# Differential attention maps in three PSUM banks, and re-costed attention plans, in a two-block fp32 network

## The chip, the cores and the metric

One core of one Trainium2 chip. The metric is device microseconds of one execution. The program is one launch of some 52,000 instructions; everything is fp32 (matmuls run on fp32 data, in part split into a high and a low fp32r half).

## The reference, cut to what matters

The network is a first block (latent attention, dilated attention, an expert-choice feed-forward) and a second block of two layers. Each layer of the second block runs three attentions over 1024 positions and 256 context positions; the one that the change touches is the differential one, with 4 heads and two maps to a head:

```python
def diff_attend(q, k, v, lam):
    s = jnp.einsum('bqhmd,bkhmd->bhmqk', q, k).astype(jnp.float32) * (q.shape[-1] ** -0.5)
    p = jax.nn.softmax(s, axis=-1)
    a = (p[:, :, 0] - lam * p[:, :, 1]).astype(v.dtype)
    return jnp.einsum('bhqk,bkhd->bqhd', a, v)

for l in range(DEPTH_2):
    ...
    oa = map_query_blocks(lambda q_blk: diff_attend(q_blk, ka_all, va_all, lam), qa)
    yb = map_query_blocks(lambda q_blk: gqa_attend(q_blk, kb_all, vb_all), qb) * jax.nn.silu(gb)
    yn = neighbourhood_attend(qn, kn, vn, kn_c, vn_c, nat_rpb[l], rows)
    y = jnp.concatenate([ya, yb, yn], axis=-1) @ w_out[l]
    if l < DEPTH_2 - 1:
        ...   # the same for the 256 context rows, of layer 0 alone
```

With 128 queries to a tile, a layer has 4 heads x 8 tiles x 2 maps = 64 maps of 128 x 1280 scores.

## The kernel before

The program runs in stages: projections of the first block, its attention (`attn1`), its output projection and router, the experts, and for each of the two layers projections (`proj2`), attention (`attn2`) and output projection (`out2`). The three attention stages are not written in the order in which they run. They are handed to a planner, class `Plan`: `Plan.op` takes a priority, a dictionary of engines with an assumed duration in us on each (of several the first one that is free in the plan is taken), the function that emits the instructions, the operations it depends on, its buffers and the time of its transfer. `Plan.run` is a list scheduler: it walks through the assumed time, starts the ready operation of lowest priority number whose engine is free and whose buffers are to be had, and emits its instructions. Each engine then executes its instructions in the order so made. A dependency between engines counts `HOP`, and a load is done 2.0 us after its transfer. So the assumed durations set the order of the instructions and the choice between engines, and nothing else.

PSUM has eight banks of 512 fp32 columns. The tags `s` (scores), `t` (transposes and transposed scores) and `o` (outputs) share them, each up to a cap from the table `TUNE`; a buffer is taken in the plan when its first operation starts and given back when its last one ends.

A layer's plan has two streams. Stream `x` (`stream_x`) runs the neighbourhood attention of three pairs of heads and then grouped-query attention of three pairs; stream `d` (`stream_d`) the four differential heads. Each stream paces its priorities with `step`; `df` in `TUNE` stretches or shortens the pace of `d` as a share of the stage, `d0` is its start, `lead` is how far ahead loads are put, `aS`, `aD` and `aN` how far ahead the scores are put, `pvx` and `pvd` how far behind the products with the values.

A differential query tile (`d_tile`, line 2010) computes two maps. Its scores go to five `s` banks: two banks of 512 columns for each map, and one bank that holds the last 256 columns of both. For each piece VectorE copies the scores to SBUF and takes their maximum at once (`copy_max`, line 1859: the scores plus a broadcast zero, with an accumulated maximum). A small reduction (line 2038) makes the negated maximum of a map out of its three pieces, and ScalarE takes the exponential of all 1280 columns in place (line 2044) with that as bias. The second map, scaled by -lambda and the ratio of the sums, is added to the first on GpSimd or VectorE (`combine`, lines 1958 to 1961); ten transposes, their evictions and the product with the values follow.

A neighbourhood tile (`nat_tile`) takes two `s` banks and up to three passes with bias and maximum on VectorE (lines 2271 and 1861). Grouped-query attention and the latent attention of the first block (`st_group`) take the maxima of scores (line 1020), then scores anew in transposed form, exponentials on ScalarE (line 1053) and a running sum of them on GpSimd or VectorE (line 1057). The weights of the output projection are loaded and split inside the plan (`out2_weights`), once all four differential heads are done, as they take the space of the heads' buffers.

Of the kernel before, what the change touches and what calls it, by code (L numbers as in the profile page):

```python
# [9 lines left out]
F32 = mybir.dt.float32  # L10
# [78 lines left out]
class Plan:  # L89
# [4 lines left out]
    HOP = 0.22  # L94
# [60 lines left out]
    def run(self):  # L155
# [5 lines left out]
        while left:  # L161
# [11 lines left out]
            for o in cand:  # L173
# [17 lines left out]
                if o.dma:  # L191
                    dma = max(end, dma) + o.dma
                    done = dma + 2.0
# [18 lines left out]
        self.span = max(max(free.values()), dma + 2.0)  # L212
# [13 lines left out]
class Kern:  # L226
# [251 lines left out]
    def matvec_ops(self, p, dur, parts):  # L478
# [6 lines left out]
        for k in range(KD):  # L485
# [3 lines left out]
            o = pl.op(q, {"pe": 1.2}, lambda e, k=k, W=W: products(O.t, W.t, k), [lw, o], [W, O])  # L489
# [445 lines left out]
    def plan(self, caps, pools, rest):  # L935

        self.pl = pl = Plan(caps, BANKS)

        def buf(tag, stream, shape=None, dt=F32):
            if tag in ("t", "o", "oT"):  # L940
                stream = None
            if tag in ("s", "t", "o"):
                return pl.buf(tag, stream, lambda i: self.ps.tile([P, 512], F32, name=self.nm(tag), tag=f"b{i}", bufs=1))
# [5 lines left out]
    def mla_pair(self, p):  # L949
# [19 lines left out]
        def part(g):  # L969
# [3 lines left out]
            for i in range(2):  # L973
# [14 lines left out]
                fins.append(self.st_group(X, 3.05, NT, CH[:2], s1, st, 0.65, [Q, K], [lq, lk], Q, lambda Q=Q: Q.t[96:100, 0, :],  # L988
# [5 lines left out]
    def st_group(self, X, dur, nb, ch, s1, st, cost, QK, lds, M, mdst, V, lv, vc, Y, yc, tagP, tagA, sm):  # L994
# [7 lines left out]
        def tile_tops(pp, j0):  # L1002
# [4 lines left out]
            def bank(parts):  # L1007
# [14 lines left out]
                o = pl.op(p - self.q["aS"], {"pe": 0.02 + n * w * 0.00042}, mm, lds, [Sb] + QK)  # L1022
                os.append(pl.op(p - self.q["aS"], {"dve": 0.07 + n * w * 0.00104}, top, [o], [Sb]))
# [8 lines left out]
            tops.append(pl.op(pp[1] - self.q["aS"], {"dve": 0.08}, fin, os))  # L1032
# [14 lines left out]
        om = pl.op(p, {"act": 0.66, "dve": 0.6}, mrows, [o] + lds, [T, M])  # L1047
        exps, acc = [], None
        for kb in range(nb):
# [3 lines left out]
            exps.append(pl.op(q, {"act": 0.48}, lambda e, kb=kb, T_=T_: nc.scalar.activation(PT.t[:, kb, :], T_.t, AF.Exp), [o], [T_, PT]))  # L1053
            if kb:
# [3 lines left out]
                acc = pl.op(q, {"pool": 1.23, "dve": 0.6}, add, [exps[kb - 1], exps[kb], acc], [PT, A])  # L1058
# [62 lines left out]
    def dil_unit(self, p, h, part, half, Q, K, lds, Y, env):  # L1121
# [15 lines left out]
        def bank(a):  # L1137
# [20 lines left out]
            o = pl.op(p - self.q["aE"], {"pe": 0.43}, scores, lds, [Sb, Q, K])  # L1158
            tops.append(pl.op(p, {"dve": 0.68}, top, [o], [Sb, Pt] + yb))
# [1332 lines left out]
```

## Time and profile before

| | us |
|---|---|
| median of the runs (3593.01 to 3593.92) | 3593.58 |
| the profiled execution | 3575.55 |
| its span, first to last instruction | 3573.6 |
| busy in the span: TensorE (matmul) | 3341.9 (94%) |
| VectorE | 2359.4 (66%) |
| ScalarE | 1703.9 (48%) |
| GpSimd | 1221.0 (34%) |

Busy shares are averages over stages with different limits; the rows further below are by stage. Matmuls are pipelined and their ends are modelled, so TensorE's share says little about its rate; where it matters, the distance from the start of one matmul to the start of the next is read.

### The profile page before, as it was taken

The numbers are of one execution on the slowest core, as the hardware profiler recorded it, in microseconds if no ns is written. First come the engines' busy times: TensorE is split into PE (matmuls) and PEld (weight loads), VectorE is DVE, ScalarE is ACT, GpSimd is POOL, SyncE is SP. The second block draws the span as 40 slices with busy tenths as digits, with TensorE's granted clock in tenths as the row PEclk, the third lists the DMA queues.
The fourth block names the chain that finished last, engine by engine and source line by source line (L and its number), as shares of the span: only waits on it lengthen the run. The fifth ranks groups of instructions, "written<-read, shape, count | busy, mean of one in ns | idle before, by whom it ended". The sixth has DMA issues, their size and how long they took to land. (4 is left out here: it accounts for less than half of the span.)

```text
span 3573.6 us, 51656 instructions
## 1 busy us (share of the span) xinstructions
PE 3341.9 (94%) x17880; PEld 2572.3 (72%) x17880; DVE 2359.4 (66%) x5555; ACT 1703.9 (48%) x3138; POOL 1221.0 (34%) x1071
## 2 busy tenths in 40 slices
PE   7998899979499999989999899999999999999999
PEld 5987666657388887779889566556899888665557
DVE  5524546444799999876850788886546813899962
ACT  4324444422388877663321676554333213766540
POOL 3211323332000101033540356665334512556551
PEclk9999999999699999999999999999999999999999
DMA  7338677565799999654451653113344444531133
GB/s 206 92 112 234 159 211 218 162 217 180 256 393 392 399 392 362 235 169 127 134 156 55 159 124 86 38 40 124 124 128 128 116 142 115 145 89 45 40 101 112
DMA packets 398650, 600.21 MB, mean 168 GB/s; under 512 B 77330, under 2 KB 281234, under 8 KB 394290
## 3 DMA queue, kind: packets, MB, share of 16 engines
q1 hardware_dynamic: 339828, 486.92, 40.7%
q0 software_dynamic: 26240, 94.13, 11.3%
q10 hardware_dynamic: 32320, 15.86, 1.6%
q8 instruction: 141, 2.31, 0.3%
q14 instruction: 121, 0.99, 0.1%
HBM read 473.33 MB, written 123.50 MB: 167 GB/s over the span
## 5 line engine op out<-in xcount | busy, mean ns | idle before, releaser
L348 PE MATMUL a<-wh,h2H 128*128 128x384 f32 (+2 forms) x1328 | 475.5, 358 | 3.5 <-ACT h2H L595 3.5
L350 PE MATMUL a<-wh,h2L 128*128 128x384 f32 (+2 forms) x1328 | 469.1, 353 | 4.4 <-POOL h2L L596 4.3
L349 PE MATMUL a<-wl,h2H 128*128 128x384 f32 (+2 forms) x1328 | 468.6, 353 | 1.7 <-DVE wl L335 1.2
L1481 DVE TENSOR_TENSOR wl<-wr,wh 128x1024 fp32r<-128x1024 f32 x384 | 450.4, 1222 | 27.3 <-ACT wh L1480 20.8
L1480 ACT ACTIVATE wh<-wr 128x1024 fp32r<-128x1024 f32 x384 | 395.9, 1059 | 78.7 <-PE s L350 78.2
L350 PEld LDWEIGHTS a<-wh,h2L 128*128 128x128 f32 x1328 | 250.9, 189 | 28.5 <-POOL h2L L596 6.4
L348 PEld LDWEIGHTS a<-wh,h2H 128*128 128x128 f32 x1328 | 251.4, 189 | 24.9 <-ACT h2H L595 4.2
L349 PEld LDWEIGHTS a<-wl,h2H 128*128 128x128 f32 x1328 | 251.4, 189 | 23.4 <-DVE wl L335 1.5
L1861 DVE CUSTOM_DVE_ANT_0 dP<-s,zero 128x512 f32<-128x512 f32 (+1 forms) x384 | 217.1, 595 | 7.9 <-PE s L2022 5.1
L349 PE MATMUL s<-wl,xH 128*128 128x512 f32 x512 | 202.0, 395 | 4.5 <-DVE wl L1481 4.2
L348 PE MATMUL s<-wh,xH 128*128 128x512 f32 x512 | 202.6, 396 | 0.0
L350 PE MATMUL s<-wh,xL 128*128 128x512 f32 x512 | 200.4, 391 | 0.0
L2044 ACT ACTIVATE dP<-dP,d 128x1280 f32<-128x1280 f32 x128 | 174.1, 1363 | 52.8 <-DVE d L2038 43.6
L1057 POOL TENSOR_TENSOR xP<-xP,xPT 128x512 f32<-128x512 f32 x118 | 164.3, 1393 | 38.8 <-DVE xP L1057 21.7
L1020 DVE TENSOR_REDUCE x<-s 128x1 f32<-128x512 f32 (+1 forms) x240 | 158.2, 684 | 24.1 <-PE s L2181 23.5
L348 PE MATMUL s<-wh,yoH 128*128 128x512 f32 x416 | 166.9, 402 | 2.7 <-ACT wh L333 1.9
L335 POOL TENSOR_TENSOR wl<-wr,wh 128x1024 fp32r<-128x1024 f32 (+3 forms) x43 | 94.1, 2189 | 217.2 <-ACT wh L333 215.1
L349 PE MATMUL s<-wl,yoH 128*128 128x512 f32 x416 | 166.0, 399 | 0.5 <-DVE wl L335 0.5
L350 PE MATMUL s<-wh,yoL 128*128 128x512 f32 x416 | 164.6, 396 | 0.0
L1053 ACT ACTIVATE xPT<-t 128x512 f32<-128x512 f32 x240 | 128.8, 604 | 71.6 <-PE t L2186 62.6
L1463 POOL DMA_INDIRECT xg<-h2d,idx x16 | 16.4, 1026 | 402.4 <-PE t L316 328.1
L335 DVE TENSOR_TENSOR wl<-wr,wh 128x1024 fp32r<-128x1024 f32 (+3 forms) x55 | 73.7, 1342 | 114.4 <-ACT wh L333 114.4
(451 smaller groups left out, 8395.1 us busy)
## 6 DMA issues: line engine op xcount, KB each, us to landing
wr<-in_w_gate_dram SPq DMA_DIRECT2D x128, 512.0 KB
wr<-in_w_up_dram SPq DMA_DIRECT2D x128, 512.0 KB
wr<-in_w_down_dram SPq DMA_DIRECT2D x128, 512.0 KB
aw<-in_w_ada_dram SPq DMA_DIRECT2D x32, 1024.0 KB
wr<-in_w_in_dram SPq DMA_DIRECT2D x44, 512.0 KB
aw<-in_w_ada_dram SPq DMA_DIRECT2D x32, 512.0 KB
xk<-stackCk POOLq DMA_DIRECT2D x24, 640.0 KB, 8.5
wr<-in_w_in_dram SPq DMA_DIRECT2D x36, 384.0 KB
```

The lines of the kernel that those rows point to most:

```text
L335: e.tensor_tensor(l, raw, h.bitcast(F32), ALU.subtract)
L348: nc.tensor.matmul(out, sH, h, start=first, stop=False)
L349: nc.tensor.matmul(out, sH, l, start=False, stop=False)
L350: nc.tensor.matmul(out, sL, h, start=False, stop=last)
L1020: nc.vector.tensor_reduce(dst, Sb.t[:, :n * w].rearrange("p (k c) -> p k c", k=n) if n > 1 else Sb.t[:, :w], AX.X, ALU.max)
L1053: exps.append(pl.op(q, {"act": 0.48}, lambda e, kb=kb, T_=T_: nc.scalar.activation(PT.t[:, kb, :], T_.t, AF.Exp), [o], [T_, PT]))
L1057: eng.tensor_tensor(A.t[:, :512], PT.t[:, 0, :] if kb == 1 else A.t[:, :512], PT.t[:, kb, :], ALU.add)
L1463: nc.gpsimd.indirect_dma_start(out=xg, out_offset=None, in_=self.h2[:, :], in_offset=bass.IndirectOffsetOnAxis(ap=self.idx[:, e:e + 1], ax ...
L1480: nc.scalar.activation(h, raw, AF.Copy)
L1481: nc.vector.tensor_tensor(l, raw, h.bitcast(F32), ALU.subtract)
L1861: self.nc.vector.tensor_tensor_reduce(dst, src, self.zero.to_broadcast(list(src.shape)), 1.0, -3e38, ALU.add, ALU.max, m)
L2044: nc.scalar.activation(Ps[i].t, Ps[i].t, AF.Exp, bias=b["m"][:, i:i + 1], accum_out=box[j][:, i:i + 1])
```

## The change

Three things are changed. A differential map gets one PSUM tile of three banks (tag `w`, one of them; `s`, `t` and `o` share the five that remain in the layers), and VectorE takes it out in one pass of 1280 columns, negated, with the minimum of the negated scores accumulated; the exponential uses a scale of -1 and that minimum as its bias. The planner's assumed durations are replaced in nearly all operations, `HOP` becomes 0.25 and the time to a load's landing 5.0. And the table `TUNE` has new values for all three stages. The first block's attention gets no `w` tile and keeps its eight shared banks.

```diff
 TUNE = {
-    "first": dict(lead=15, aS=38, aE=17.5, st=0.07, pvm=10, pve=6.6, m0=15, d0=22, df=0.89, a0=60, ad=50, **{"as": 55}, s=6, t=3, o=1),
-    0: dict(lead=15, aS=28.3, aD=0, aN=10.0, st=0.0, pvx=28.1, pvd=16.4, d0=28.0, df=0.7, s=4, t=4, o=2),
-    1: dict(lead=27.4, aS=30.8, aD=5.3, aN=22.1, st=0.59, pvx=29.7, pvd=34.6, d0=4.0, df=0.8, s=4, t=5, o=2),
+    "first": dict(lead=23.3, aS=87.8, aE=0, st=1.1, pvm=10.1, pve=31.4, m0=39.5, d0=22.1, df=0.886, a0=60.8, ad=66.4, **{"as": 57.1}, s=4, t=7, o=2),
+    0: dict(lead=22.2, aS=54.6, aD=15.2, aN=47.2, st=0.4, pvx=21.6, pvd=16.7, d0=37.1, df=0.53, s=2, t=6, o=6),
+    1: dict(lead=13.3, aS=103.7, aD=14.6, aN=39.8, st=0.2, pvx=28.2, pvd=79.2, d0=14.4, df=0.5, s=2, t=4, o=2),
 }
...
-    HOP = 0.22
+    HOP = 0.25
...
-                    done = dma + 2.0
+                    done = dma + 5.0
...
-        self.pl = pl = Plan(caps, BANKS)
+        self.pl = pl = Plan(caps, BANKS - 3 * caps.get("w", 0))
...
-            exps.append(pl.op(q, {"act": 0.48}, lambda e, kb=kb, T_=T_: nc.scalar.activation(PT.t[:, kb, :], T_.t, AF.Exp), [o], [T_, PT]))
+            exps.append(pl.op(q, {"act": 0.61}, lambda e, kb=kb, T_=T_: nc.scalar.activation(PT.t[:, kb, :], T_.t, AF.Exp), [o], [T_, PT]))
...
-                acc = pl.op(q, {"pool": 1.23, "dve": 0.6}, add, [exps[kb - 1], exps[kb], acc], [PT, A])
+                acc = pl.op(q, {"pool": 1.4, "dve": 1.1}, add, [exps[kb - 1], exps[kb], acc], [PT, A])
...
-        return {"act": 0.06 + n * 0.00083, "dve": 0.07 + n * 0.00104}
+        return {"act": 0.18 + n * 0.00083, "dve": 0.15 + n * 0.00104}
...
-            return pl.op(p, {"pool": n * 0.00325, "dve": 0.13 + n * 0.00104}, f, [dep], [P0] if P0 is P1 else [P0, P1])
+            return pl.op(p, {"pool": 0.1 + n * 0.0033, "dve": 0.15 + n * 0.0014}, f, [dep], [P0] if P0 is P1 else [P0, P1])
...
     def d_tile(self, pp, j, Q, K, lds, Ps, box, sm):
-        b, tops, last = {}, ([], []), []
...
-        for parts in [[(0, c0, w)] for c0, w in CH[:2]] + [[(0, *CH[2]), (1, *CH[2])]] + [[(1, c0, w)] for c0, w in CH[:2]]:
-            bank(parts)
+        last = []
         for i in range(2):
...
+            W, p, m = buf("w", "d"), pp[i], {}
+
+            def mm(e, i=i, W=W):
+                for c0, w in CH:
+                    nc.tensor.matmul(W.t[:, c0:c0 + w], Q.t[:, i, j * P:(j + 1) * P], K.t[:, i, c0:c0 + w], start=True, stop=True)
+
+            def top(e, i=i, W=W, m=m):
+                m["m"] = sm(1)
+                nc.vector.tensor_tensor_reduce(Ps[i].t, W.t[:, :1280], self.zero.to_broadcast([P, 1280]), -1.0, 3e38, ALU.add, ALU.min, m["m"])
+
+            def exps(e, i=i, m=m):
                 if j not in box:
                     box[j] = self.slots(2)
...
+                nc.scalar.activation(Ps[i].t, Ps[i].t, AF.Exp, bias=m["m"], scale=-1.0, accum_out=box[j][:, i:i + 1])
+            o = pl.op(p - self.q["aD"], {"pe": 0.71}, mm, lds, [W, Q, K])
+            o = pl.op(p, {"dve": 0.24 + 1280 * 0.00104}, top, [o], [W, Ps[i]])
+            last.append(pl.op(p, {"act": 0.49 + 1280 * 0.00083}, exps, [o], [Ps[i]]))
         return last
```

## Rows read from the trace of the kernel before

**Rows 1.** Busy time by stage: stretch and length, each engine, clock, DMA share, GB/s.

```profile
346.00:767.00 421.00, 386.09 (x2287) 253.04 (x2286) 222.31 (x584) 191.01 (x510) 152.81 (x144) 0.95 0.68 190
1988.00:2476.00 488.00, 468.21 (x2587) 293.09 (x2583) 419.81 (x1215) 306.17 (x623) 290.36 (x267) 0.97 0.33 85
2999.00:3470.00 471.00, 448.78 (x2479) 279.02 (x2479) 408.18 (x1201) 290.89 (x548) 278.01 (x248) 0.97 0.36 92
```

**Rows 2.** VectorE by line, layer 1, 2999 to 3470: count, busy, mean ns, idle.

```profile
L1861 DVE CUSTOM_DVE_ANT_0 dP<-s,zero 128x512 f32<-128x512 f32 x128 | 85.1, 683 | 2.3 <-PE s L2022 1.7
L1057 DVE TENSOR_TENSOR xP<-xP,xPT 128x512 f32<-128x512 f32 x37 | 45.2, 1224 | 1.3
L1861 DVE CUSTOM_DVE_ANT_0 dP<-s,zero 128x256 f32<-128x256 f32 x64 | 24.3, 417 | 0.0
L1861 DVE DVE_READ_ACCUMULATOR2_ANT d<- 128x1 f32 x192 | 15.9, 83 | 0.0
L1958 DVE SCALAR_TENSOR_TENSOR dP<-dP,d,dP 128x1280 f32<-128x1280 f32 x8 | 14.8, 1856 | 0.0
L2038 DVE TENSOR_REDUCE d<-d 128x1 f32<-128x3 f32 x64 | 9.8, 152 | 1.0
```

**Rows 3.** VectorE's timeline in layer 1: start, duration, instruction.

```profile
3053.94 0.69 DVE L1861 CUSTOM_DVE_ANT_0 dP<-s,zero 128x512 f32<-128x512 f32 x1
3054.55 0.69 DVE L1861 CUSTOM_DVE_ANT_0 dP<-s,zero 128x512 f32<-128x512 f32 x1
...
3057.77 0.41 DVE L1861 CUSTOM_DVE_ANT_0 dP<-s,zero 128x256 f32<-128x256 f32 x1
...
3058.11 0.42 DVE L1861 CUSTOM_DVE_ANT_0 dP<-s,zero 128x256 f32<-128x256 f32 x1
...
3058.52 0.68 DVE L1861 CUSTOM_DVE_ANT_0 dP<-s,zero 128x512 f32<-128x512 f32 x1
```

**Rows 4.** TensorE's timeline in layer 1, at two places: start, duration, instruction.

```profile
3182.80 0.50 PE L2022 MATMUL s<-dk,dq 96*128 96x512 f32 x1
3183.13 0.27 PE L316 MATMUL t<-ident,xP 128*128 128x128 f32 x1
...
3405.01 0.39 PE L2185 MATMUL t<-xq,xk 128*128 128x512 f32 x1
3405.24 0.40 PE L2186 MATMUL t<-tb,xk 68*128 68x512 f32 x1
```

**Rows 5.** VectorE by line, first block's output projection, 767 to 900.

```profile
L1340 DVE TENSOR_TENSOR yo<-s,gt_bc 128x1024 f32<-128x1024 f32 x7 | 8.6, 1225 | 25.6 <-PE s L350 25.6
```

**Rows 6.** TensorE's waits, first block's attention: us in total, times, longest.

```profile
PE s L980 <- DMA mq<-stackMq: 14.8, 6, 7.0
PE s L467 <- DMA aw<-in_w_ada_dram: 6.2, 2, 4.5
```

**Rows 7.** DMA issues, first block's attention: count, KB each, median us to landing.

```profile
mq<-stackMq POOLq DMA_DIRECT2D x16, 384.0 KB, 5.8
```

**Rows 8.** Busy time in ten microseconds at the end of layer 0 and layer 1.

```profile
2460.00:2470.00 10.00, 8.93 (x42) 4.77 (x40) 9.90 (x7) 7.71 (x13) 9.77 (x6) 1.00 0.44 136
3460.00:3470.00 10.00, 4.40 (x22) 3.59 (x19) 2.81 (x3) 2.60 (x3) 3.81 (x4) 0.68 0.84 277
```

**Rows 9.** ScalarE and GpSimd by line, layer 1, 2999 to 3470.

```profile
L1053 ACT ACTIVATE xPT<-t 128x512 f32<-128x512 f32 x120 | 64.5, 602 | 40.4 <-PE t L2186 37.4 <-POOL xy L2170 2.1
L1057 POOL TENSOR_TENSOR xP<-xP,xPT 128x512 f32<-128x512 f32 x59 | 82.0, 1391 | 15.3 <-DVE xP L1057 6.3 <-ACT xPT L1053 5.8
L1871 POOL DMA_DIRECT2D dq<-stackAq x24 | 13.0, 548 | 43.2 <-PE a L350 35.5 <-PE s L2022 5.2 <-PE s L2181 2.1
```

**Rows 10.** Layer 1 in two parts, and the heads' exponentials: min/median/max ns, first and last start.

```profile
3000.00:3200.00 200.00, 195.43 (x1255) 132.81 (x1253) 173.55 (x669) 145.03 (x277) 103.82 (x120) 0.99 0.56 134
3200.00:3470.00 270.00, 252.97 (x1225) 145.89 (x1224) 234.43 (x532) 145.37 (x271) 173.50 (x128) 0.96 0.22 60
L2044 ACT ACTIVATE dP<-dP,d x64: 1350/1363/1392, 3017.1 to 3401.7; 128x1280 f32<-128x1280 f32 x64
```

More of the change, by code (lines that the diff above doesn't have):

```diff
@@ L935, in plan @@
     def plan(self, caps, pools, rest):
-        self.pl = pl = Plan(caps, BANKS)
+        self.pl = pl = Plan(caps, BANKS - 3 * caps.get("w", 0))
         def buf(tag, stream, shape=None, dt=F32):
-            if tag in ("t", "o", "oT"):
+            if tag in ("t", "o", "oT", "w"):
                 stream = None
+            if tag == "w":
+                return pl.buf(tag, stream, lambda i: self.ps.tile([P, 1536], F32, name=self.nm(tag), tag=f"w{i}", bufs=1))
             if tag in ("s", "t", "o"):
@@ L1031, in fin @@
                 nc.vector.tensor_reduce(b["m"][:, j0:j0 + 2], x["m2"].rearrange("p (j r) -> p j r", j=2), AX.X, ALU.max, negate=True)
-            tops.append(pl.op(pp[1] - self.q["aS"], {"dve": 0.08}, fin, os))
+            tops.append(pl.op(pp[1] - self.q["aS"], {"dve": 0.16}, fin, os))
         pp = [self.step(X, dur) for j in range(4)]
@@ L1157, in top @@
                                                    ALU.add, ALU.max, m4()[:, j:j + 1])
-            o = pl.op(p - self.q["aE"], {"pe": 0.43}, scores, lds, [Sb, Q, K])
-            tops.append(pl.op(p, {"dve": 0.68}, top, [o], [Sb, Pt] + yb))
+            o = pl.op(p - self.q["aE"], {"pe": 0.9 if part == "B" else 0.5}, scores, lds, [Sb, Q, K])
+            tops.append(pl.op(p, {"dve": 1.0}, top, [o], [Sb, Pt] + yb))
         bank(0)
@@ L1169, in exps @@
                 nc.scalar.activation(Pt.t[:, j, :], Pt.t[:, j, :], AF.Exp, bias=b["n"][:, j:j + 1], accum_out=d4()[:, j:j + 1])
-        o = pl.op(p, {"dve": 0.07}, neg, tops, yb)
-        o = pl.op(p, {"act": 1.97}, exps, [o], [Pt] + yb)
+        o = pl.op(p, {"dve": 0.17}, neg, tops, yb)
+        o = pl.op(p, {"act": 2.7}, exps, [o], [Pt] + yb)
         evs = []
@@ L1935, in pv_halves @@
         o = pl.op(p, {"pe": 1.7 if den else 0.8}, back, [o] + (den[0] if den else []), [oT, T] + (den[2] if den else []))
-        return pl.op(p, {"dve": 0.33 + (0.09 if den else 0)}, lambda e: fin(T.t[:, :256].rearrange("p (j d) -> p j d", d=64), T.t[:, 256:260]),
+        return pl.op(p, {"dve": 0.43 + (0.16 if den else 0)}, lambda e: fin(T.t[:, :256].rearrange("p (j d) -> p j d", d=64), T.t[:, 256:260]),
                      [o], [T] + fin.bufs)
@@ L2012, in d_tile @@
         nc, pl, buf = self.nc, self.pl, self.buf
-        b, tops, last = {}, ([], []), []
-        def bank(parts):
-            Sb = buf("s", "d")
-            i0, _, w = parts[0]
-            n = len(parts)
-            def mm(e):
-                for k, (i, c0, w) in enumerate(parts):
-                    nc.tensor.matmul(Sb.t[:, k * w:(k + 1) * w], Q.t[:, i, j * P:(j + 1) * P], K.t[:, i, c0:c0 + w], start=True, stop=True)
-            def top(e):
-                if "m2" not in b:
-                    b["m2"], b["m"] = sm(6), sm(2)
-                for k, (i, c0, w) in enumerate(parts):
-                    r = 3 * i + c0 // 512
-                    self.copy_max(Ps[i].t[:, c0:c0 + w], Sb.t[:, k * w:(k + 1) * w], b["m2"][:, r:r + 1])
-            o = pl.op(pp[i0] - self.q["aD"], {"pe": 0.02 + n * w * 0.00042}, mm, lds, [Sb, Q, K])
-            o = pl.op(pp[i0], {"dve": n * (0.07 + w * 0.00104)}, top, [o], [Sb] + [Ps[i] for i, _, _ in parts])
-            for i, _, _ in parts:
-                tops[i].append(o)
@@ L2169, in gated @@
     def gated(self, p, o, Y, G_, lg, cs):
[L2170 removed]
+        return self.pl.op(p, {"pool": 0.84}, lambda e: self.nc.gpsimd.tensor_tensor(Y.t[:, :, cs], Y.t[:, :, cs], G_.t[:, :, cs], ALU.mult),
                           [o, lg], [Y, G_])
@@ L2272, in f @@
                                                ALU.add, ALU.max, x["m2"][:, r:r + 1])
-            return pl.op(p, {"dve": 0.07 + w * 0.00104}, f, [os[a], lt], [Sb[a], TB, Pt])
+            return pl.op(p, {"dve": 0.24 + w * 0.00104}, f, [os[a], lt], [Sb[a], TB, Pt])
         def context(e):
```

35 lines of the change are left out of this document (14 added, 21 removed).

## The prediction

> **What bounds the kernel now.** I read the busy time by stage first. The plans that the change re-orders run in three stretches: attention of the first block (421 us), attention of layer 0 (488 us) and of layer 1 (471 us), together 1380 us of the 3573.6 [rows 1]. The reader is to see two things there. TensorE is listed as busy for 92 to 96% of each, but matmul ends are modelled, so that is no proof of work at its rate. And in both layers VectorE is nearly as full: 419.81 of 488 and 408.18 of 471 us, 86 and 87%, against 222.31 of 421 in the first block [rows 1]. So a layer has two engines near their limit that feed each other in a fixed order, and the first block has one.
>
> Then the groups of VectorE by line, for layer 1. The differential maxima are its largest item: 128 wide pieces 85.1 us, 64 narrow ones 24.3, 192 accumulator reads 15.9 and 64 small reductions 9.8, in all 135.1 us [rows 2]. The timeline shows what a piece costs the queue, which is less than its duration, since the next one starts before it ends: a wide piece takes 0.61 us from start to start, a narrow one 0.34, and a narrow one with the small reduction behind it 0.41, so that the reduction adds 0.07 [rows 3].
>
> Last, TensorE's timeline, for what one busy number hides: in an unbroken run of 512-column matmuls one starts every 0.23 us, while a lone differential piece with a transpose behind it holds the engine 0.33 us [rows 4]. Breaking a run costs about 0.10 us.
>
> **The change part by part.** *A, the maxima.* Per query tile five score banks, six maxima and two reductions become two three-bank tiles with one 1280-column maximum each; the negated minimum needs no reduction. No 1280-column pass out of PSUM stands in the trace. The nearest is a 1024-column one out of two banks, 1225 ns [rows 5]; against the 683 ns of 512 columns [rows 2] that is 1.06 ns a column, and no loss at the bank's edge. So 1225 + 256 x 1.06 = 1496 ns, plus the read of 83 ns. By durations a layer falls from 135.1 to 64 x 1.58 = 101 us, 34 less. By starts a tile falls from 4 x 0.61 + 2 x 0.34 + 2 x 0.07 = 3.26 to 2 x 1.42 = 2.84 us (1.49 less the 0.07 by which neighbours overlap), and 32 tiles give 13 us. Bounds for two layers: 27 to 68 us of VectorE. I take the lower, as starts are what the queue feels, and three quarters of it, because the engine is at 87% and not 100: **-20 us**; between 0 and -68.
>
> The Trainium skill (Perfetto Trace Analysis, Optimizing Scalar/DVE Operations) puts the overhead that VectorE pays per instruction on PSUM at about 125 ns, and advises grouping where the engine is saturated. By that figure a map that goes from three passes to one saves 0.25 us, an estimate of 32 us for both layers before the reductions, close to my lower bound. The same section says that where an engine is not saturated but makes others wait, breaking instructions up may be better; which of the two holds at 87% is the question of the first rival.
>
> The wide maximum adds a wait: it starts when the third matmul of its map has ended, and whatever stands behind it in VectorE's queue (evictions of transposes, the neighbourhood's biased maxima) waits with it. With one three-bank tile the next map's matmuls wait for it in turn. By the rates above a map takes 0.23 + 0.23 + about 0.12 of TensorE, 1.50 and 0.08 of VectorE, some 2.2 us and the hops; 64 of them are 140 us of a 471 us stage. The single tile does not bind by itself.
>
> *A2, the matmuls.* 160 pieces a layer become 64 runs of three. Up to 96 breaks go, at 0.10 us [rows 4]: at most 10 us a layer if all stood alone, nothing if the old plan already put them together. I take half: **-10 us** for both; between 0 and -19.
>
> *B, landings.* The planner now lets a load land 5.0 us after its transfer instead of 2.0. In the first block TensorE waits 14.8 us for mq and 6.2 for the ada weights [rows 6]; mq lands a median of 5.8 us after issue [rows 7], so 5.0 is nearer the truth, and the leads grow from 15 to 23.3. Half of the 21.0: **-10 us**; between 0 and -21.
>
> *C, the ends.* The weights of the output projection are loaded only when all differential heads are done. At the end of layer 1 TensorE works 4.40 of 10 us, at the end of layer 0 8.93 of 10, 6.7 us idle in all [rows 8]. A head stream that is paced over 0.5 to 0.53 of the stage instead of 0.7 to 0.8 frees the space in mid stage, and the splits are done by the end. **-5 us**; between 0 and -7. What moves with the heads are their loads, 24 dq issues of 548 ns a layer on GpSimd among them [rows 9], ahead of its adds; their number is the same, and the DMA engines are at a third of their time in these stages [rows 1]. I cost that at nothing; without that cover it is 13 us a layer.
>
> *D, the order.* The old costs leave out work: in layer 1, 120 exponentials of 602 ns are planned at 480 (15 us), 59 GpSimd adds of 1391 at 1230 (9 us) [rows 9], 37 VectorE adds of 1224 at 600 (23 us) and 8 combines of 1856 at 1461 (3 us) [rows 2]: 50 us a layer by which engines run later than the plan thinks, and with in-order queues whatever was placed behind them is late too. No row shows how much of that TensorE pays. The bounds are all of it returned, -100 us for two layers, and a new order that fits worse, +20 us, as much as I credit it. I take a fifth: **-20 us**. For the first block I count only B.
>
> Sum: -20 - 10 - 10 - 5 - 20 = -65 us. The profiled execution took 3575.55 us; 3575.55 - 65 = 3510.6. The median of the runs is 3593.58, 18.0 above the profiled one, and I carry that over: **3529 us**.
>
> **The rivals.** *First, slower: the wide maximum stands in the neighbourhood's way.* In layer 1 the heads' exponentials run from 3017.1 to 3401.7, four fifths of the stage; at df 0.5 they are pressed into its first half, where the neighbourhood tiles run, and VectorE is already busy 173.55 of the first 200 us [rows 10]. A neighbourhood tile holds two score banks at once, and the cap on them goes from four to two, with five banks left for everything but the maps. So the next tile's scores can't start until VectorE has passed whatever stands ahead; a 1.49 us maximum there in place of a 0.61 us piece is 0.88 us. If each of the 48 tiles of a layer meets one and TensorE has nothing else due, that is 42 us a layer, 84 for both: 3529 + 84 = 3613. It decides from 65/96 = 0.68 us a tile. For it: 87% in that window. Against it: in the second part VectorE is at 234.43 of 270 [rows 10] and has room to catch up once the heads are gone, and the score matmuls are planned far ahead (aN 39.8 to 47.2). The skill's same page (Matmul Optimizations) asks that all eight PSUM banks be used; three banks that lie idle once the heads are done go against it, and this price is what that would mean here.
>
> *Second, no change: what is freed is hidden.* TensorE's own work fills the stages, A, A2 and D return nothing, B a quarter and C half, 2.5 us each: 3589.
>
> *Third, the pass does not do what it says*: 1280 columns against a broadcast operand run no faster than the other 1280-column VectorE pass of the trace, 1856 ns [rows 2]. Then a layer's maxima take 64 x 1.94 = 124 us by durations, 11 less than now instead of 34, so A shrinks to a third, -7: 3542.
>
> *Fourth, more: the plan was the limit.* D returns 60 instead of 20, and A three quarters of the 68 us by durations, 51 instead of 20: 3529 - 40 - 31 = 3458.
>
> **How the numbers follow.** Forecast 0.52 (its own range 3495 to 3565), slower 0.20, no change 0.09, a slow pass 0.06, more 0.13. A measurement of this kernel can tell about 0.2%, 7 us, from no change. Faster takes the forecast, the slow pass and the fourth: 0.71; same 0.09; slower 0.20. The range reaches from just under the fourth rival's 3458 to just over the first one's 3613: 3452 to 3620.
>
> **What would show it.** A: the groups of VectorE show 64 passes of 128x1280 a layer at 1.45 to 1.55 us, and no small reduction at the differential tops; VectorE's busy time in a layer falls by 15 us or more. A2: the differential score matmuls stand in threes. B: the wait for mq in the first block is under 8 us. C: the last 10 us of layer 1 are full. D: each layer's stage is 20 to 35 us shorter, the first block's about 10. If the first half of a layer grows while its second shrinks, and TensorE's waits name the maxima of line 1861's successor ahead of score matmuls, the first rival holds. What would make this wrong above all is D: the plan's order is not in the trace, and its sign is the least certain of the five.

## The result and the profile after

The changed kernel takes 3546.62 us (median of 4 runs, 3542.28 to 3547.95) beside 3593.30 (3587.74 to 3593.92) for the kernel before: 0.987 of it, 95% interval 0.985 to 0.989. The forecast was 3529, its range 3452 to 3620; the direction and the range held. Of its five terms only the one for the ends came out near its size.

The profiled execution of the changed kernel took 3546.51 us, 29 less than the profiled one of before, and not 47, since that one lay 18 us under its own median. For the comparisons below every stage is cut at marks that any of the kernels has: from the start of the last projection matmul ahead of an attention to the start of the first output-projection matmul behind it, rounded to a microsecond (so a length in the table further below can differ by one from the stretch shown here). Busy time by these stages, first block, layer 0 and layer 1 (columns as in [rows 1]); first the kernel before,

```profile
331.00:773.00 442.00, 398.55 (x2355) 264.28 (x2354) 233.73 (x619) 200.27 (x527) 154.85 (x148) 0.94 0.69 191
1962.00:2484.00 522.00, 490.93 (x2722) 312.61 (x2721) 436.10 (x1276) 319.40 (x647) 302.88 (x292) 0.96 0.37 95
2999.00:3473.00 474.00, 451.78 (x2493) 282.02 (x2493) 410.15 (x1204) 292.52 (x551) 278.74 (x249) 0.97 0.37 93
```

then the changed one:

```profile
331.00:757.00 426.00, 393.23 (x2351) 261.18 (x2349) 232.36 (x620) 198.52 (x529) 160.21 (x153) 0.95 0.70 197
1948.00:2477.00 529.00, 491.91 (x2721) 314.17 (x2719) 408.44 (x953) 319.69 (x642) 330.97 (x304) 0.95 0.37 92
2994.00:3444.00 450.00, 438.89 (x2494) 281.68 (x2492) 364.91 (x859) 299.55 (x562) 300.51 (x266) 0.99 0.39 98
```

The third busy column is VectorE. It falls by 28 us in layer 0 and by 45 in layer 1. Layer 0 is 7 us longer all the same, layer 1 is 24 shorter, and the first block, which has no wide tile at all, is 15 shorter. So the relief of VectorE and the time do not go together. Of the 24 us of layer 1, 13 are less busy time of TensorE and 11 less idle time; in layer 0 TensorE's idle time grew by 6 us. VectorE's wide maxima by line, layer 1 of the changed kernel, which answer to [rows 2]:

```profile
L2027 DVE CUSTOM_DVE_ANT_0 dP<-w,zero 128x1280 f32<-128x1280 f32 x64 | 95.0, 1484 | 6.4 <-PE w L2023 5.8 <-POOL dP L1964 0.3
L2027 DVE DVE_READ_ACCUMULATOR2_ANT d<- 128x1 f32 x64 | 5.3, 82 | 0.0
```

The wide pass does what the sum said, 1484 ns and a read of 82 ns; 135.1 us of maxima became 100.3. The differential score matmuls, before and after, by line, layer 1:

```profile
L2022 PE MATMUL s<-dk,dq 96*128 96x512 f32 (+1 forms) x192 | 67.5, 405 | 2.4 <-DVE x L1020 1.5 <-DVE d L1861 1.0
```

```profile
L2023 PE MATMUL w<-dk,dq 96*128 96x512 f32 (+1 forms) x192 | 52.9, 383 | 0.9 <-DVE d L2027 0.8
```

The same 192 matmuls occupy TensorE 14.6 us less. TensorE's waits in the first block's attention (us in total, times, longest), which answer to [rows 6]:

```profile
PE s L467 <- DMA aw<-in_w_ada_dram: 7.8, 3, 3.5
...
PE s L983 <- DMA mq<-stackMq: 4.3, 2, 3.2
```

The wait for mq fell from 14.8 to 4.3 us, that for the ada weights did not fall. Ten microseconds before the ends of both layers, at the places of [rows 8]:

```profile
2453.00:2463.00 10.00, 10.00 (x44) 5.39 (x45) 7.00 (x7) 8.39 (x15) 7.82 (x6) 1.00 0.23 65
3431.00:3441.00 10.00, 7.65 (x42) 5.56 (x42) 5.98 (x8) 2.71 (x3) 5.34 (x4) 0.83 0.97 366
```

TensorE is idle 2.3 us of the twenty instead of 6.7. The heads' exponentials in layer 1, which answer to the last of [rows 10]:

```profile
L2032 ACT ACTIVATE dP<-dP,d x64: 1348/1363/1384, 3013.7 to 3348.6; 128x1280 f32<-128x1280 f32 x64
```

They run for 335 us of a 450 us stage, 385 of 474 before. The heads do end earlier, 95 us ahead of the stage's end where it was 71, but they are far from pressed into its first half, as the prediction had them at df 0.5.

### The profile page after: what moved, and what is told of

It is laid out like the page before. It is cut to its first block, busy times and chain, and to the rows that moved or that the text cites. A ratio compares the mean times of both kernels' runs of the same rounds, so it can differ in the third digit from the quotient of the medians.

```text
span 3544.7 us, 51023 instructions
## 1 busy us (share of the span) xinstructions
PE 3326.8 (94%) x17880; PEld 2572.9 (73%) x17880; DVE 2281.2 (64%) x4889; ACT 1709.8 (48%) x3145; POOL 1277.3 (36%) x1107
## 4 chain that ended last, share of the span: by engine, by line
PE 62%; DVE 7%; DMA 2%; POOL 2%; issue 2%; ACT 1%; SPq 0%; ACTq 0%; DVEq 0%; POOLq 0%
PE s L349 7%; PE s L350 7%; PE s L348 7%; PE t L316 6%; PE a L350 6%; PE a L349 6%; PE a L348 6%; PE o L1929 5%; PE o L2211 2%; PE w L2023 2%; PE s L2171 2%; PE s L2254 2%; PE t L2175 1%; PE t L2176 1%; PE t L1937 1%
## 5 line engine op out<-in xcount | busy, mean ns | idle before, releaser
L1060 POOL TENSOR_TENSOR xP<-xP,xPT 128x512 f32<-128x512 f32 x134 | 189.4, 1415 | 54.6 <-ACT xPT L1056 33.2
L2027 DVE CUSTOM_DVE_ANT_0 dP<-w,zero 128x1280 f32<-128x1280 f32 x128 | 189.9, 1484 | 15.7 <-PE w L2023 9.8
```

Of the source, the lines that this page charges most:

```text
L1060: eng.tensor_tensor(A.t[:, :512], PT.t[:, 0, :] if kb == 1 else A.t[:, :512], PT.t[:, kb, :], ALU.add)
L2027: nc.vector.tensor_tensor_reduce(Ps[i].t, W.t[:, :1280], self.zero.to_broadcast([P, 1280]), -1.0, 3e38, ALU.add, ALU.min, m["m"])
```

## The experiments

The first theory was the prediction's: the tile relieves the engines, and truer durations make a better order, each by itself. Its rival: the parts only go together. A table of all kernels stands at the end of this section.

**e1_tile: the tile alone.** `d_tile`, the `w` tag and its banks are the change's; costs and table are those of before.

```diff
-        self.pl = pl = Plan(caps, BANKS)
+        self.pl = pl = Plan(caps, BANKS - 3 * caps.get("w", 0))
...
+                nc.vector.tensor_tensor_reduce(Ps[i].t, W.t[:, :1280], self.zero.to_broadcast([P, 1280]), -1.0, 3e38, ALU.add, ALU.min, m["m"])
```

> The three-bank tile alone, with the old table and the old assumed durations (the tile's own operations costed by the old rule). Stages are counted from the last projection matmul to the first one of the output projection: before 442 / 522 / 474 us (first block, layer 0, layer 1), the change 427 / 529 / 450. Theory 1 (the tile relieves VectorE and TensorE, the order does the rest): the first block stays at 442, the two layers are 10 to 18 us shorter each (half of A plus half of A2). Theory 2 (the tile takes banks from the other stream, and the new plan made up for that in layer 1 alone): both layers are 5 to 20 us longer than before.

**e2_costs: the durations alone.** Here and below, "durations" stands for the assumed durations together with `HOP` and the time to a load's landing.

```diff
-    HOP = 0.22
+    HOP = 0.25
...
-                    done = dma + 2.0
+                    done = dma + 5.0
...
-                acc = pl.op(q, {"pool": 1.23, "dve": 0.6}, add, [exps[kb - 1], exps[kb], acc], [PT, A])
+                acc = pl.op(q, {"pool": 1.4, "dve": 1.1}, add, [exps[kb - 1], exps[kb], acc], [PT, A])
...
```

> The new assumed durations, hop and landing alone, with the old table and five score banks. Theory 1 (accurate durations make a better order by themselves): each of the three stages is 5 to 15 us shorter. Theory 2 (the table's numbers were found for one set of durations and go with it): the stages move by up to 15 us with either sign, and the sum is near nothing or worse than before.

**e3_table: the table alone.**

```diff
-    1: dict(lead=27.4, aS=30.8, aD=5.3, aN=22.1, st=0.59, pvx=29.7, pvd=34.6, d0=4.0, df=0.8, s=4, t=5, o=2),
+    1: dict(lead=13.3, aS=103.7, aD=14.6, aN=39.8, st=0.2, pvx=28.2, pvd=79.2, d0=14.4, df=0.5, s=2, t=4, o=2),
...
```

> The new table alone, with the old assumed durations and five score banks. Theory 1: near the time of before, since the order's gain needs the durations. Theory 2 (table and durations go together): worse than before by 10 us or more in the layers, all the more as the cap of two score banks now also holds for the five banks of a differential tile.

**e4_tile_costs: tile and durations, the old table.** The edits of e1_tile and e2_costs together.

> The tile and the new durations, with the old table: the change without its table. Theory 1: most of the change's time is there, 430 / 515 / 455 us. Theory 2: the gain of layer 1 (450) is the table's, so layer 1 stays above 462 here; and if layer 0's loss (529 against 522) is the table's, layer 0 is under 522 here.

Measured: 3750.48, 3683.41, 3789.18 and 3728.73 us, beside 3583.82 for the kernel before. No part, nor the tile and the durations together, does anything but harm, 100 to 205 us of it, and the prediction's theory of separate gains falls. The second theories were nearer, but two of them missed the size by far: e1_tile was to lose 5 to 20 us a layer and lost 67 and 100, e2_costs was to move each stage by up to 15 us and lost 98 in layer 0; and layer 0 of e4_tile_costs, which was to be under 522 us if the table made the change's loss there, took 585. For the tile alone the trace shows where. Busy time by stage of e1_tile, layer 0 and layer 1, and TensorE's waits in layer 1:

```profile
1972.00:2561.00 589.00, 518.12 (x2724) 328.36 (x2723) 413.42 (x961) 319.77 (x637) 319.53 (x299) 0.93 0.34 85
3074.00:3648.00 574.00, 491.72 (x2497) 312.92 (x2495) 374.21 (x868) 302.41 (x558) 286.01 (x255) 0.90 0.29 75
```

```profile
PE t L316 <- DVE xPT L1860: 18.0, 29, 0.9
PE t L316 <- ACT dPT L1858: 14.1, 24, 1.1
PE t L316 <- ACT xPT L1858: 9.9, 17, 0.8
PE w L2023 <- DVE d L2027: 8.2, 12, 1.4
PE t L316 <- DVE dPT L1860: 6.2, 10, 0.8
```

VectorE is as relieved as in the changed kernel (374 us in layer 1). But TensorE's transposes (line 316) wait 80 times, 48.2 us, each time for the eviction of an earlier transpose, as if they had too few banks to go through. That is 48 of the 60 us by which TensorE is idle longer than before in this layer; the other 40 us of the loss are its own busy time, 492 us at a mean granted clock of 0.90 beside 452 at 0.97. With three of eight banks given to the maps, the old cap of four lets the scores hold four of the other five. That gave the theory for the next kernels: the caps on the shared banks decide whether the tile pays.

**e8_tile_caps: e1_tile with the new caps and nothing else.** The diff is against the kernel before; in layer 1 only the caps of `s` and `t` differ, and that of `t` falls.

```diff
-    0: dict(lead=15, aS=28.3, aD=0, aN=10.0, st=0.0, pvx=28.1, pvd=16.4, d0=28.0, df=0.7, s=4, t=4, o=2),
-    1: dict(lead=27.4, aS=30.8, aD=5.3, aN=22.1, st=0.59, pvx=29.7, pvd=34.6, d0=4.0, df=0.8, s=4, t=5, o=2),
+    0: dict(lead=15, aS=28.3, aD=0, aN=10.0, st=0.0, pvx=28.1, pvd=16.4, d0=28.0, df=0.7, s=2, t=6, o=6),
+    1: dict(lead=27.4, aS=30.8, aD=5.3, aN=22.1, st=0.59, pvx=29.7, pvd=34.6, d0=4.0, df=0.8, s=2, t=4, o=2),
```

> The tile alone, with all of the old table and costs kept but the caps on shared banks in the two layers, which are those of the new table (layer 0: s 2, t 6, o 6; layer 1: s 2, t 4, o 2). Theory caps: bank starvation was nearly all of the slowdown of the tile alone (3750.48), so the two layers fall back to about the kernel before's 522 and 474 us, less some relief of VectorE: 3550 to 3610. Theory fit: the paces of the old table do not suit the tile whatever the caps: 3650 or more.

Measured: 3554.77 us, beside 3584.45 for the kernel before. Busy time, layer 0 and layer 1:

```profile
1968.00:2478.00 510.00, 483.40 (x2723) 310.88 (x2721) 413.61 (x947) 323.24 (x660) 305.98 (x289) 0.97 0.39 99
2993.00:3451.00 458.00, 443.11 (x2496) 283.39 (x2494) 376.35 (x876) 296.29 (x555) 269.27 (x249) 0.98 0.38 94
```

Of the transposes' waits for the eviction of a transpose, 48.2 us in e1_tile's layer 1, these are left:

```profile
PE t L316 <- DVE dPT L1860: 0.2, 1, 0.2
PE t L316 <- DVE xPT L1860: 0.2, 1, 0.2
```

The theory of the caps holds: five numbers of the table turn a loss of 167 us into a gain of 30, and all of it lies in the two layers. In layer 1 it must be the cap on the scores, since that of the transposes went down; in layer 0 three caps changed at once. The old paces and the old costs go well with the tile. What the new caps do without the tile, with the maxima in pieces and all eight banks shared, was not run.

**e6_tile_table: the change without its durations.** Tile and table are the change's, costs, `HOP` and landing the old ones.

> The change without the new durations: three-bank tiles and the new table, but the planner's old costs, HOP 0.22 and landing 2.0 (the wide maximum is planned by the old formula, 0.07 + 1280 x 0.00104). Theory caps: the tile alone was slow (3750.48) because its plan let the scores hold four of the five shared banks; the new table's cap of two cures that, and the durations add little: 3540 to 3600. Theory fit: the table's paces were chosen for an order that the durations make; without them the order misses by as much as it did with other pairs of parts: 3640 to 3760.

Measured: 3592.91 us. Busy time, all three stages:

```profile
332.00:799.00 467.00, 418.23 (x2355) 271.26 (x2355) 231.70 (x618) 200.05 (x540) 155.19 (x149) 0.90 0.64 180
1990.00:2508.00 518.00, 482.50 (x2725) 308.71 (x2723) 414.77 (x954) 322.19 (x648) 319.96 (x292) 0.97 0.37 96
3022.00:3490.00 468.00, 446.23 (x2496) 282.92 (x2494) 380.73 (x870) 298.54 (x552) 272.75 (x249) 0.97 0.37 94
```

In the band of the caps, but by a sum of unlike parts: against the change the durations (with the landing) are worth 40 us in the first block and 18 in layer 1, and layer 0 is better off without them by 11.

**e7_pieces: the wide pass taken back at a fixed order.** The plan, and so the order on all engines, is the change's.

```diff
-                m["m"] = sm(1)
-                nc.vector.tensor_tensor_reduce(Ps[i].t, W.t[:, :1280], self.zero.to_broadcast([P, 1280]), -1.0, 3e38, ALU.add, ALU.min, m["m"])
+                m["m"], m["m2"] = sm(1), sm(3)
+                for r, (c0, w) in enumerate(CH):
+                    self.copy_max(Ps[i].t[:, c0:c0 + w], W.t[:, c0:c0 + w], m["m2"][:, r:r + 1])
+                nc.vector.tensor_reduce(m["m"], m["m2"], AX.X, ALU.max, negate=True)
...
-                nc.scalar.activation(Ps[i].t, Ps[i].t, AF.Exp, bias=m["m"], scale=-1.0, accum_out=box[j][:, i:i + 1])
+                nc.scalar.activation(Ps[i].t, Ps[i].t, AF.Exp, bias=m["m"], accum_out=box[j][:, i:i + 1])
```

> The changed kernel with its plan untouched, so that the order on every engine and all banks are the same; only the maximum of a differential map is taken as three passes of 512, 512 and 256 columns out of the three-bank tile, with the small reduction behind them. A map then costs VectorE 0.61 + 0.61 + 0.34 + 0.07 = 1.63 us from start to start instead of some 1.42, by rows of the kernel before: 0.21 us x 128 maps = 27 us more for VectorE. Theory relief: at a fixed order VectorE's time shows, half of it or more: 3560 to 3590. Theory hidden: other engines set the pace at this order, and the wide pass gives nothing by itself: 3540 to 3552.

Measured: 3549.10 us (3538.44 to 3553.69), 0.989 of before, 0.987 to 0.992; the changed kernel's interval is 0.985 to 0.989. Busy time of layer 1, and VectorE by line in it:

```profile
2987.00:3441.00 454.00, 439.21 (x2497) 279.43 (x2495) 381.73 (x1179) 300.12 (x562) 299.49 (x266) 0.99 0.38 97
```

```profile
L1864 DVE CUSTOM_DVE_ANT_0 dP<-w,zero 128x512 f32<-128x512 f32 x128 | 82.9, 684 | 4.7 <-PE w L2023 3.3 <-POOL dP L1964 0.8
L1864 DVE CUSTOM_DVE_ANT_0 dP<-w,zero 128x256 f32<-128x256 f32 x64 | 26.8, 419 | 0.0
L2029 DVE TENSOR_REDUCE d<-d 128x1 f32<-128x3 f32 x64 | 10.0, 156 | 2.2
```

The pieces are back, at the durations of [rows 2], and VectorE is busy 17 us longer in layer 1 and 21 in layer 0. The time differs by 2.5 us, within the 15 us over which e7_pieces itself spreads. The profiled stages are a little finer: layer 1 took 453.7 us, where the four other kernels with this plan (the change, e9, e10 and e12) took 449.9 to 451.0, and layer 0 took 532 beside 529 and 526. So 3 to 6 us a layer, at most 10 in all, may be the relief's (the first block, which has no such pass, came out 4 us shorter and hides some of that in the time). The rest of it, the reason for which one would make this change, is hidden. This holds for the change's order; at the old paces the pass was not taken apart from the rest. The Trainium skill (Perfetto Trace Analysis, Optimizing Scalar/DVE Operations) expects larger, grouped operations to help an engine that is saturated, and says that breaking them up may help where an engine is not saturated but makes others wait. Here, at 81 to 84% busy in this layer, the times with and without grouping lie within the spread, so these runs bear out neither.

**e11_reserved: three banks of their own, but no whole map.** The kernel before, with the pieces of the differential scores in three reserved one-bank buffers and the caps of e8 in layer 1. In layer 0 its caps are t 4 and o 2, where e8 has t 6 and o 6.

```diff
...
+            if tag == "w":
+                return pl.buf(tag, stream, lambda i: self.ps.tile([P, 512], F32, name=self.nm(tag), tag=f"w{i}", bufs=1))
...
-            Sb = buf("s", "d")
+            Sb = buf("w", "d")
```

> The kernel before with one change: the pieces of the differential scores get three banks of their own, one 512-column bank to a piece, in a separate tag, and the other tags share the remaining five with the caps of e8_tile_caps (s 2; t 4, o 2). Maxima stay in pieces, five to a query tile; old costs, old paces. e8 with the whole-map tile took 3554.8, the kernel before 3584.5 in that call. Theory separation: what pays is that the heads' scores no longer compete with the neighbourhood's and the transposes for banks: 3550 to 3565. Theory whole map: what pays is the map in one piece (three matmuls in a run, one wait and one pass instead of five of each): 3578 to 3610.

Measured: 3602.56 us, beside 3581.89. Busy time, layer 0 and layer 1, and the score matmuls of layer 1 by line:

```profile
1965.00:2508.00 543.00, 504.76 (x2718) 309.19 (x2717) 424.92 (x1279) 316.21 (x639) 313.50 (x295) 0.95 0.37 93
3021.00:3499.00 478.00, 457.48 (x2494) 282.52 (x2493) 403.50 (x1215) 286.55 (x534) 259.58 (x244) 0.97 0.36 90
```

```profile
L2024 PE MATMUL w<-dk,dq 96*128 96x512 f32 (+1 forms) x192 | 70.0, 414 | 2.7 <-DVE d L1863 2.1
```

and the same matmuls in e8_tile_caps:

```profile
L2023 PE MATMUL w<-dk,dq 96*128 96x512 f32 (+1 forms) x192 | 53.0, 385 | 2.4 <-DVE d L2027 2.3
```

Setting banks apart brings nothing; the whole map is what pays, 20 us in layer 1 between this kernel and e8. The 34 us in layer 0 are not the map's alone, as two caps differ there too. At the change's order e7 showed that the pass on VectorE is worth little. If that holds at the old paces, which no run tells, it is what e7 keeps: the three matmuls of a map in one run, and two operations of a kind for the planner to place to a pair of maps instead of five. In layer 1 the score matmuls' busy time differs by 17.0 us, and TensorE's as a whole by 14.4 of the 20; the rest is idle time. No run splits matmul runs and planning further.

**e12_landing: the first block planned with the old landing.** The last line stands in `attn1`.

```diff
+    LAND = 5.0
...
-                    done = dma + 5.0
+                    done = dma + self.LAND
...
+        pl.LAND = 2.0
```

> The changed kernel with one number put back: in the first block's plan a load lands 2.0 us after its transfer, as in the kernel before, instead of 5.0; its new row and durations and both layers are the change's. From the last projection matmul to the first output projection the first block's attention took 427, 422 and 426 us in the three profiles with the change's plan, 442, 450 and 449 in the three with the old one. Theory landing: the gain is that the plan foresees the loads, and it goes: 440 or more, 3560 to 3570 in all. Theory order: it is the longer lead, the row and the durations of the operations: 420 to 430, 3540 to 3552.

Measured: 3585.50 us, beside 3581.89. Busy time of the first block's attention, and TensorE's waits in it:

```profile
329.00:798.00 469.00, 414.69 (x2354) 271.93 (x2352) 233.81 (x613) 199.38 (x541) 162.28 (x155) 0.91 0.65 179
```

```profile
PE s L985 <- DMA mq<-stackMq: 15.9, 7, 4.8
PE s L468 <- DMA aw<-in_w_ada_dram: 14.2, 5, 5.9
```

The one number costs 43 us there, far more than its theory asked for: the waits for mq and the ada weights go from 12.1 to 30.1 us by these rows, and TensorE's busy time grows by 21, at a mean granted clock of 0.91 beside 0.95. That the plan then places the other work worse too is the likely reason, but it was not taken apart. The landing is not enough by itself either. Four fields are filled for this stage: old row and old landing 442 to 450 us (before, e1, e8, e11), old row and new landing 444 and 445 (e2, e4), new row and old landing 461 to 469 (e3, e6, e12), both new 422 to 427 (the change, e7, e9, e10, e13).

**e9_mix: layer 0 wholly as in the kernel before.** `KernB` is that kernel's class with its own table and planner.

```diff
+        if l == 0:
+            mine, self.__class__ = self.__class__, KernB
+            self.attn2_open(l)
+            self.__class__ = mine
+            return
```

> The changed kernel, but layer 0's attention is planned and computed as in the kernel before (old table row, old costs, five score banks to a query tile); the first block and layer 1 are the change's. By the two profiles layer 0 went from 522 to 529 us and layer 1 from 474 to 450. Theory layer 0 lost: the stages are independent, and the time is the changed kernel's less 3 to 12 us: 3534 to 3544. Theory noise: layer 0's difference is execution to execution variation, or is given back in the next stage: within 3 us of the changed kernel, 3543 to 3550.

Measured: 3538.49 us (3534.39 to 3539.25), 8 under the changed kernel; the ranges do not meet, and the first theory's band holds. But of the 7 us between the two profiled executions only 3 lie in layer 0 (526 beside 529), and e12_landing, which has the change's layer 0, took 526 there as well; the kernel before took 522. So layer 0 gained nothing by the change; that it lost is likely, and not shown by this run.

**e10_layer0: layer 0 as in e8_tile_caps.** The same edit, with e8's class.

> The changed kernel, but layer 0 is planned as in e8_tile_caps: three-bank tiles, the old costs and paces, the new caps (s 2, t 6, o 6). First block and layer 1 are the change's. In its one look e8 had 510 us from the last projection matmul of layer 0 to its first output projection, the changed kernel 529, the kernel before 522. Theory parts add: 3546.6 - 19 = 3527, between 3520 and 3535, below the changed kernel and below e9_mix (3538.5). Theory chance: e8's 510 was a good execution, and layer 0 comes out near e9's 526: 3536 to 3546.

Measured: **3523.55 us** (3523.01 to 3524.38), 0.985 of before, 0.983 to 0.986; 23 under the changed kernel, and faster than both. Busy time, all three stages:

```profile
331.00:756.00 425.00, 394.33 (x2357) 260.93 (x2355) 232.82 (x623) 199.30 (x530) 160.17 (x153) 0.95 0.70 198
1943.00:2453.00 510.00, 482.48 (x2726) 310.02 (x2725) 414.31 (x948) 323.15 (x660) 305.83 (x289) 0.97 0.39 100
2971.00:3421.00 450.00, 438.88 (x2495) 281.76 (x2493) 365.34 (x859) 299.71 (x562) 300.68 (x266) 0.99 0.39 98
```

Each stage comes out as in the kernel that it was taken from: 425 beside 426, 510 beside 510, 450 beside 450. Stages add. Layer 0's 19 us against the change are half TensorE's idle time (37 us there, 27.5 here) and half its busy time (492 and 482 us, at mean granted clocks of 0.95 and 0.97).

**e13_old_paces: the change with the layers' old paces and the new caps.** It tells whether the durations or the paces lost layer 0.

```diff
-    0: dict(lead=22.2, aS=54.6, aD=15.2, aN=47.2, st=0.4, pvx=21.6, pvd=16.7, d0=37.1, df=0.53, s=2, t=6, o=6),
+    0: dict(lead=15, aS=28.3, aD=0, aN=10.0, st=0.0, pvx=28.1, pvd=16.4, d0=28.0, df=0.7, s=2, t=6, o=6),
...
```

> The changed kernel, but the rows of the table for both layers have the paces of the kernel before with the new caps (as in e8_tile_caps); the new durations, HOP and landing stay. It fills the fourth field of a square in each layer, all with three-bank tiles and new caps: old durations and old paces took 510 us in layer 0 and 458 in layer 1 (e8), old durations and new paces 518 and 468 (e6), new durations and new paces 529 and 450 (the change). Theory paces: the new paces are what lost layer 0 and the durations are harmless: 505 to 514 in layer 0, about 455 in layer 1, 3520 to 3535 in all. Theory durations: with the new durations the planner finds a worse order for layer 0 whatever the paces: 521 to 535 there, 3540 to 3560 in all.

Measured: 3568.45 us, beside 3578.41. Busy time, layer 0 and layer 1:

```profile
1948.00:2483.00 535.00, 493.14 (x2726) 311.40 (x2724) 410.67 (x951) 317.52 (x642) 331.58 (x306) 0.95 0.36 91
2999.00:3463.00 464.00, 443.84 (x2496) 282.45 (x2494) 371.47 (x870) 290.62 (x539) 286.71 (x259) 0.98 0.35 89
```

The time is 8 us above the second theory's band, layer 0 at its upper end. In layer 0 it is the durations: 25 us with the old paces (510 to 535), 11 with the new (518 to 529). In layer 1 they cost 6 with the old paces and give 18 with the new. Why truer durations give a worse order in layer 0 was not tried, nor were `HOP` and the landing taken apart from them in the layers. One difference that goes with it: they send more combines to GpSimd, where the add alone takes 2.97 us against 1.5 to 2.0 for the whole on VectorE (26 of the long ones in layer 0 of the change, 21 in e10's); but e6 has 26 too and took 518.

All kernels, with the stages in us (one profiled execution each; a stage with the same plan repeats within 8 us in the first block and 5 in a layer) and the time. What a profiled execution takes outside of the three stages is 2136 to 2145 us in all fourteen, so to within 9 us the difference between two kernels lies in these stages:

| kernel | maps | durations | paces | caps | first block | layer 0 | layer 1 | time |
|---|---|---|---|---|---|---|---|---|
| before | pieces | old | old | old | 442 | 522 | 474 | 3593.3 |
| e1_tile | whole | old | old | old | 450 | 589 | 574 | 3750.5 |
| e2_costs | pieces | new | old | old | 445 | 620 | 477 | 3683.4 |
| e3_table | pieces | old | new | new | 461 | 668 | 522 | 3789.2 |
| e4_tile_costs | whole | new | old | old | 444 | 585 | 563 | 3728.7 |
| e8_tile_caps | whole | old | old | new | 449 | 510 | 458 | 3554.8 |
| e6_tile_table | whole | old | new | new | 467 | 518 | 468 | 3592.9 |
| e13_old_paces | whole | new | old (first block new) | new | 425 | 535 | 464 | 3568.5 |
| the change | whole | new | new | new | 427 | 529 | 450 | 3546.6 |
| e7_pieces | whole, max in pieces | new | new | new | 422 | 532 | 454 | 3549.1 |
| e12_landing | whole | new, old landing in the first block | new | new | 469 | 526 | 451 | 3585.5 |
| e11_reserved | pieces, reserved | old | old | new | 445 | 544 | 478 | 3602.6 |
| e9_mix | layer 0 as before | | | | 426 | 526 | 450 | 3538.5 |
| e10_layer0 | layer 0 as e8 | | | | 425 | 509 | 450 | 3523.6 |

## Why the prediction was right, and where it was not

The range and the sign held because the first block and the whole maps gave more than they were given credit for, and so paid for two terms that gave next to nothing or less. Those two, A and D, were 40 of the forecast's 65 us; that the number came within 18 us is luck.

**A (forecast -20).** The pass was costed right, 1496 ns against 1484 and 101 us a layer against 100.3, and the third rival, a pass at 1856 ns, is refuted. The step that failed is "three quarters of it, because the engine is at 87%": the share of a freed engine's time that becomes kernel time. It was at most 10 us for both layers (e7), where the forecast was 20. Here the second rival's reason holds: most of what is freed was hidden. VectorE at 81 to 84% busy was no bound at the change's order; layer 0, 28 us lighter on VectorE, grew.

**A2 (forecast -10, bound -19).** The mechanism held and the size was wrong, bound included. 96 breaks at 0.10 us were allowed for. Summed from each score matmul's start to the next start on TensorE, in layer 1 the 192 of them hold the engine 53.3 us before and 43.5 after; they stand in 126 runs before and in 64 after. So 62 breaks gave 9.8 us of TensorE's time, 0.16 each (in layer 0 it is 58.8 and 46.7 us, in 124 and 64 runs), not the 0.10 that was read from a single break [rows 4]. The reading itself had the wrong side: the piece at 3182.80 lost its 0.10 us not to the transpose behind it but to the products with the values ahead of it. The kernel before, layer 1:

```profile
3123.93 0.65 PE L2221 MATMUL o<-xPT,xv 128*64 128x256 f32 x4
3124.52 0.49 PE L2022 MATMUL s<-dk,dq 96*128 96x512 f32 x1
3124.94 0.43 PE L2221 MATMUL o<-xPT,xv 128*64 128x128 f32 x2
...
3182.21 0.65 PE L2221 MATMUL o<-xPT,xv 128*64 128x256 f32 x4
```

Over this layer's 512-column pieces the median from start to next start is 0.43 us between two products (14 pieces), 0.34 behind a product and ahead of a transpose (4), 0.32 behind a transpose and ahead of one (9), but 0.24 behind other heads' scores and ahead of a transpose (10), and 0.23 between two other pieces (6). So a piece pays some 0.10 us when a product stands ahead of it, 0.08 when a transpose does, and 0.09 when a product stands behind it; a transpose behind it, or other scores on either side, cost nothing. By busy time the gain is 14.6 us, and 17 in e11 against e8. The whole map as one operation of the plan, by which these two kernels differ, was worth 20 in layer 1; the prediction had no term for a plan that has to place five pieces with five waits instead of two.

**B (forecast -10, bound -21).** Right in its mechanism, but half of the size: 422 to 427 us against 442 to 450, some 20. The wait for mq came under 8 us, as was to be seen. The two waits together account for 9 of the 15 us between the two profiled executions. The bound was not one: in the new order a landing of 2.0 costs 43 us (e12), of which the two waits are 18. And the old row with the new landing gains nothing (e2, e4), so the landing is half of a pair.

**C (forecast -5).** The ends gave 4.4 us of idle time back, though the last 10 us of layer 1 are at 7.65 and not full. And the reason was only partly the one named: heads did not end in mid stage at df 0.5, only 24 us further from the end.

**D (forecast -20, bounds -100 to +20).** The sign failed. Each layer was to be 20 to 35 us shorter; layer 0 is 7 longer. With the tile and the new caps in place, new durations and paces together cost 19 us in layer 0 (510 to 529) and give 8 in layer 1 (458 to 450): +11. The 50 us a layer by which the old costs fell short were read rightly from [rows 2, 9], but "late in the plan's eyes" is not "late on the chip": the queues run at their own pace, and the durations only decide the order. e13 and e6 show that truer durations help or harm by the paces that stand beside them.

**What was missed.** The caps on the shared banks were read as a danger. The first rival said that two score banks instead of four would hold up the neighbourhood's scores; e1 and e8 show the reverse: with four the transposes lack banks and the tile costs 167 us, with two it gains 30. In the changed kernel TensorE waits 3.7 us in layer 0 and 0.8 in layer 1 for a wide maximum ahead of the maps' own score matmuls, where that rival wanted 42 a layer. The fourth rival, three times the gain from the order, falls with D's sign.

**The sum.** Tile with new caps, in the two layers: -12 and -16 (522 to 510, 474 to 458). First block: about -20. Durations and paces in the layers: +19 and -8. Together -37, where the kernel before was measured at 3578.4 to 3584.5 in the later comparisons, 32 to 38 above the changed kernel; the median of 3593.3 in the comparison with the change is 47 above it, and no profile shows the 10 us more. The 18 us that were carried over from the profiled execution to the median belong to the kernel before's own spread: its single executions ran from 3571.89 to 3600.18, and what sets that was not found. The 7 us that the prediction took as the least to be told from no change are too few for this kernel.

## What to carry to other kernels

A freed engine's time counts only where the others wait for it in the order at hand: keep the order fixed, take the saving back, and measure; here 17 to 21 us of VectorE in a layer came to 6 at most, while whole maps, with their runs of matmuls and fewer operations to place, came to 20 in layer 1. When a resource is cut (eight banks to five), look at every cap that was set against the old number before judging the cut, as five numbers were worth 196 us here. A planner's durations, its paces and its caps are one setting: change them stage by stage, and keep for each stage the best, since the stages added here: each of e10's came out within 2 us of the kernel that it was taken from.

## What the runs showed of the hardware

A VectorE pass over 1280 fp32 columns in three PSUM banks costs 1484 ns, in line with two banks [rows 5]: no loss at a bank's edge. From start to start it holds VectorE 1.41 us (the change, layer 1). A break in a run of 512- and 256-column fp32 matmuls cost 0.16 us on the average of 62; a 512-column one held TensorE 0.23 us among its like and 0.43 between two products with the values. mq's landing, a median of 5.8 us in [rows 7], was 9.9 in the changed kernel,

```profile
mq<-stackMq POOLq DMA_DIRECT2D x16, 384.0 KB, 9.9
```

while TensorE's wait for it fell from 14.8 to 4.3 us: the time to landing alone says nothing of who waits. Why the landing takes longer was not tried.
